# Small loads of the first stage issued behind the first weights, and one square sum moved to ScalarE

## Chip, cores and metric

The kernel runs on one core of one Trainium2 chip. The metric is the time of one execution in device microseconds (us); the median of several runs is quoted. TensorE is called PE, VectorE DVE, ScalarE ACT, GpSimd POOL, and SyncE, which issues the transfers, SP.

## The reference

A trunk of two residual layers over 256 tokens of width 1024. Only the start of it matters here:

```python
cond = jax.nn.silu(c)
cos_b, sin_b = rope_tables(positions, MOBA_DH)      # rotary tables, 64 frequencies
cos_c, sin_c = rope_tables(positions, MLA_ROPE)     # 32 frequencies
mod = cond @ mod_w[layer] + mod_b[layer]            # six vectors of 1024
sh1, sc1, g1, sh2, sc2, g2 = jnp.split(mod[:, None, :], 6, axis=-1)
h = rmsnorm(x, norm_mix[layer]) * (1.0 + sc1) + sh1
y = hybrid_mixer(h, ...)                            # h @ w_in, convolution, gated DeltaNet, attention
x = x + g1 * y
...
```

rmsnorm needs the sum of squares of every token's row. After the mixer each layer has a large expert stage (PEER), which takes most of the time and which nothing here touches.

## The kernel before, in words

Tokens lie in two tiles of 128 partitions (`self.x[:, 0]` and `self.x[:, 1]`). The **first stage** computes the squares (line 1723), the norm, and the shift and scale vectors, in four quarters `q` of the width. A quarter loads two blocks of the modulation matrix with `mods` (1 MB each, line 1696, tile `mw`, six buffers) and one block of the input weights with `fetch` (1 MB, line 790, tile `wraw`, two buffers). DVE reduces the modulation blocks (line 353). Each weight block is split into a high part `whi` by ACT and a low part `wlo` by DVE (both line 131); `quarter` makes the normalised activations `hT` (lines 234 to 250), and PE multiplies three times for each product (lines 135 to 137).

`small` is a 64 KB load of biases and gains. `sincos` (lines 886 to 917), called twice, loads frequencies and positions with four small transfers (lines 895, 896) and reduces the angles with 50 instructions on POOL (lines 898 to 916). What it returns are the Sin activations (line 917), four instructions on ACT, which are issued after the last quarter, ahead of the **hybrid stage** (the mixer). There ACT also evaluates the convolution taps (line 1117) and splits the small gate weights `t<-t` that PE multiplies first with an 8-wide stationary operand.

In the first stage SP, PE, DVE and ACT run in the order in which the code is written. In the hybrid stage a scheduler puts the instructions of each engine in order by its own estimate of when their inputs are ready; so what is written in the first stage also moves the order of the hybrid stage. Each engine executes its own list strictly in that order. Reducing the modulation blocks of later sub-layers (line 353, tile `raw`, three buffers, loaded at line 365) is spread over the hybrid stage. SP has eight semaphores for transfers that it uses in turn, so a transfer is issued only when the eighth before it has landed.

Of the kernel before, what the change touches and what calls it, by code (L numbers as in the profile page):

```python
# [16 lines left out]
OP = mybir.AluOpType  # L17
AX = mybir.AxisListType

P = 128  # L20
D = 1024
KD = D // P
S = 256
TT = S // P
# [43 lines left out]
class Trunk:  # L68
# [222 lines left out]
    def tail(self, products, add, nxt, tmp):  # L291


        def run(g):
            for _ in g:
                pass
        run(products(0, 0))
        run(products(0, 1))
        run(add(0, 0))
        run(add(0, 1))  # L300
        nxt.norm(0)
        run(products(1, 0))
        p = products(1, 1)
        next(p)
        squares = add(1, 0)
        next(squares)
        nxt.turn(0)
        run(p)
        nxt.make(0, tmp, squares)
        run(add(1, 1))  # L310
# [1330 lines left out]
    def run(self, out):  # L1641
        nc = self.nc
        self.hp = self.ctx.enter_context(self.pool("h"))
        self.st = self.ctx.enter_context(self.pool("st", side="right"))
        right, late = ExitStack(), ExitStack()
        self.order = ExitStack()
        start = ExitStack()
        start.enter_context(self.in_order("SP", "PE", "DVE", "Activation"))
        self.consts()

        def open_weights(sets):
            self.sets = sets
            self.wp = right.enter_context(self.pool(f"wp{self.n}", side="right"))

        def before_mla():
            open_weights(2)
            ml = late.enter_context(self.pool("ml0", side="right"))
            self.gate = self.t(ml, [P, D])
            mods = self.mods_in(ml, 2, *((1, p) for p in range(3, 5)))

            def ready():
                r.early = [self.weights(self.a["w1"][:, c * 2048:c * 2048 + 2048], KD, 256) for c in (2, 0)]
                r.early.append(self.load(self.a["w1"][:, 2048:4096], WMAX))
            return mods, ready

        def before_end():
            def ready():
                nc.sync.dma_start(self.fnorm, self.a["final_norm"][None, :].to_broadcast([P, D]))
            ml = late.enter_context(self.pool("ml1", side="right"))
            self.gate, self.fnorm = (self.t(ml, [P, D]) for _ in range(2))  # L1670
            return iter(()), ready

        open_weights(3)
        r = Bag()
        with self.pool("hc") as hc:
            r.row = self.t(hc, [P, D])
            r.cs = self.t(hc, [P, TT, 2, 64])
            r.cw = self.t(hc, [P, 12, 4])
            r.onorm = self.t(hc, [P, P])
            r.wba = self.t(hc, [P, KD * 8])  # L1680
            r.small = self.t(hc, [P, 2, 4])
            e = self.entry(0, 0, self.ss4)
            cond = self.t(hc, [P, KD])
            nc.sync.dma_start(cond, self.a["condc"])
            for i in range(TT):
                nc.sync.dma_start(self.x[:, i], self.a["x"][i * P:(i + 1) * P])
            nc.scalar.activation(cond, cond, AF.Silu)
            self.row_of(r.row, cond)
            with self.pool("mod") as mp, start:
                def tmp():  # L1690
                    return self.t(mp, [P, 512], tag="ent", bufs=4)

                def mods(q, c, pm=None):

                    w = self.t(mp, [P, 2, D], tag="mw", bufs=6)
                    nc.sync.dma_start(w, self.a["mod0"][q, c // 8])
                    self.mod_tile(0, c, w[:, 0], r.row)
                    if pm is None:
                        self.mod_tile(0, c + 1, w[:, 1], r.row)
                        return  # L1700
                    for k in range(KD):
                        nc.tensor.matmul(pm[:, c // 8:c // 8 + 1], w[:, 1, k * P:(k + 1) * P], cond[:, k:k + 1],
                                         start=k == 0, stop=k == KD - 1)

                def bias(c, pm=None):
                    self.mod_bias(0, c, 2 if pm is None else 1)
                    if pm is not None:
                        nc.vector.tensor_add(self.modc[0][:, c + 1:c + 2], pm[:, c // 8:c // 8 + 1],
                                             self.modb[:, 0, c + 1:c + 2])

                def product(ps, c, j, w, q):
                    f = self.proj_n if c >= 2 else self.proj_t
                    n = (256,) if c >= 2 else ()
                    f(ps, w, e.hT, KD, *n, j, ks=range(2 * q, 2 * q + 2), w0=2 * c)

                def products(q, cs):
                    for c in cs:
                        for j in range(2):
                            product(sums[c], c, j, w, q)

                for i in range(TT):
                    sq = self.t(mp, [P, D], tag="sq")
                    nc.vector.scalar_tensor_tensor(sq, self.x[:, i], 1.0, self.x[:, i], op0=OP.mult, op1=OP.mult,
                                                   accum_out=self.ss4[:, i, :1])
                e.norm(0, 1)
                e.turn(0, (0,))
                e.turn(1, (0,))
                sums = [self.out_t() for _ in range(4)]
                w = None
                for q in range(4):  # L1730
                    pm = self.ps()
                    mods(q, 8 + 2 * q, pm)
                    if not q:
                        nc.sync.dma_start(self.small, self.a["small"])
                        turns = self.sincos(r.cs, 64, self.a["freq_b"]) + self.sincos(self.cs1, 32, self.a["freq_c"])
                    else:
                        products(q - 1, (1, 2, 3))
                    if q < 3:
                        w, steps = self.fetch(self.a["w0start"][q], KD, 256)
                        for f in steps:  # L1740
                            f()
                    mods(q, 2 * q)
                    bias(2 * q)
                    bias(8 + 2 * q, pm)
                    if q == 3:
                        w, steps = self.fetch(self.a["w0start"][q], KD, 256, 4)
                    last = e.quarter(q, tmp)
                    if q < 3:
                        products(q, (0,))
                    if q == 1:  # L1750
                        e.turn(0, (1,))
                        e.turn(1, (1,))
                for f in steps:
                    f()
                early = [(Begun(sums[c], lambda j, c=c: j or products(3, (c,))), []) for c in range(4)]
                nc.sync.dma_start(r.wba, self.a["w0ba"])
                nc.sync.dma_start(r.cw, self.a["conv"])
                nc.sync.dma_start(r.small, self.a["gdn_small"][None].to_broadcast([P, 2, 4]))
                nc.sync.dma_start(r.onorm, self.a["o_norm"][None, :].to_broadcast([P, P]))
                early.append(self.fetch(self.a["w0"][6], KD, 256))  # L1760
                early.append(self.fetch(self.a["w0"][5], KD, 256))
            with self.pool("hybrid") as m, self.tc.issue_after(last[0].ins), self.tc.issue_after(last[1].ins):
                for f in turns:
                    f()
                e1 = self.entry(0, 1, self.ss4)
                first = self.hybrid(m, e.hT, r, early, self.mods(r.row, self.raw, (0, 2), (0, 3), (0, 4)), self.ss4, e1)
        e2 = self.entry(1, 0, self.ss2)
        self.peer(0, e1, first, right, ((0, 5), (1, 0)), ((1, 1), (1, 2)), before_mla, e2, self.ss2)
        late.close()
        e3 = self.entry(1, 1, self.ss4)  # L1770
        with self.pool("mla") as m:
            first = self.mla(m, e2, r.early, self.cs1, self.ss4, e3)
        end = self.finish(out)
        self.peer(1, e3, first, right, ((1, 5),), (), before_end, end, self.ss2)
        end.norm(1)
        self.order.close()
        late.close()
        right.close()
# [112 lines left out]
```

## Time and profile before

| | us |
|---|---|
| median of 3 runs | 1911.29 (1910.82 to 1915.98) |
| the profiled execution | 1913.79 |
| its span in the trace | 1912.0 |
| PE busy | 1875.2 (98%) |
| DVE busy | 1532.6 (80%) |
| ACT busy | 951.4 (50%) |
| POOL busy | 51.4 (3%) |

The span runs from the first to the last instruction in the trace; 1.8 us of the profiled execution lie around it. A share of busy time is a mean over all stages: PE at 98% is still idle for most of the first 22 us.

### The profile page before, as it was taken

The numbers are of one execution on the slowest core, as the hardware profiler recorded it, in microseconds if no ns is written. First come the engines' busy times: TensorE is split into PE (matmuls) and PEld (weight loads), VectorE is DVE, ScalarE is ACT, GpSimd is POOL, SyncE is SP. The second block draws the span as 40 slices with busy tenths as digits, with TensorE's granted clock in tenths as the row PEclk, the third lists the DMA queues.
The fourth block names the chain that finished last, engine by engine and source line by source line (L and its number), as shares of the span: only waits on it lengthen the run. The fifth ranks groups of instructions, "written<-read, shape, count | busy, mean of one in ns | idle before, by whom it ended". The sixth has DMA issues, their size and how long they took to land.

```text
span 1912.0 us, 36008 instructions
## 1 busy us (share of the span) xinstructions
PE 1875.2 (98%) x14368; PEld 1716.0 (90%) x14368; DVE 1532.6 (80%) x3265; ACT 951.4 (50%) x1309; POOL 51.4 (3%) x131
## 2 busy tenths in 40 slices
PE   6999999999999999999999999999999999999998
PEld 6999899999999888877879899999999988888886
DVE  7879789998987789878657668999778878985565
ACT  3866555454444444445545765545444444444453
POOL 7000000000000000000000000000000000000000
PEclk9999999999999999999999999999999999999999
DMA  8556575558755555589742445565554555556573
GB/s 324 177 177 236 194 276 187 200 192 281 243 173 175 174 176 175 176 279 325 231 150 111 153 184 204 180 207 186 179 177 169 175 178 177 175 182 199 192 229 102
DMA packets 97080, 376.67 MB, mean 197 GB/s; under 512 B 11920, under 2 KB 12176, under 8 KB 90256
## 3 DMA queue, kind: packets, MB, share of 16 engines
q1 hardware_dynamic: 96912, 374.37, 57.4%
q8 instruction: 112, 1.84, 0.4%
q14 instruction: 56, 0.46, 0.1%
HBM read 373.28 MB, written 1.05 MB: 196 GB/s over the span
## 4 chain that ended last, share of the span: by engine, by line
PE 77%; DVE 10%; DMA 7%; ACT 4%; issue 2%; SPq 0%; ACTq 0%; DVEq 0%
PE ps L783 26%; PE ps L626 21%; PE ps L628 11%; DMA raw<-in_v_dram 4%; DVE lo L131 3%; PE ps L649 3%; PE ps L135 3%; PE ps L137 3%; PE ps L136 3%; DMA t<-in_modT_dram 2%; PE ps L736 1%; ACT hi L131 1%; DVE t L353 1%; PE ps L323 1%; PE ps L1207 1%
## 5 line engine op out<-in xcount | busy, mean ns | idle before, releaser
L131 ACT CAST hi<-raw 128x1024 fp32r<-128x1024 f32 x508 | 534.4, 1054 | 741.8 <-PE ps L626 301.1
L131 DVE TENSOR_TENSOR lo<-raw,hi 128x1024 fp32r<-128x1024 f32 x508 | 619.2, 1221 | 233.6 <-ACT hi L131 231.0
L626 PE MATMUL ps<-hT,hi 128*128 128x256 f32 x4096 | 513.1, 278 | 2.0 <-ACT hi L131 2.0
L626 PEld LDWEIGHTS ps<-hT,hi 128*128 128x128 f32 x4096 | 484.6, 188 | 2.5 <-ACT hi L131 2.4
L628 PE MATMUL ps<-hT,lo 128*128 128x256 f32 x2048 | 275.7, 277 | 1.3 <-DVE lo L131 1.2
L783 PE MATMUL ps<-hi,vwh 128*128 128x512 f32 x976 | 266.5, 394 | 2.9 <-ACT hi L131 2.6
L783 PE MATMUL ps<-lo,vwh 128*128 128x512 f32 x976 | 261.8, 390 | 0.4 <-DVE lo L131 0.3
L783 PE MATMUL ps<-hi,vwl 128*128 128x512 f32 x976 | 261.3, 389 | 0.0
L628 PEld LDWEIGHTS ps<-hT,lo 128*128 128x128 f32 x2048 | 251.9, 188 | 2.6 <-DVE lo L131 2.3
L783 PEld LDWEIGHTS ps<-lo,vwh 128*128 128x128 f32 x976 | 182.6, 188 | 40.5 <-DVE lo L131 2.8
L783 PEld LDWEIGHTS ps<-hi,vwl 128*128 128x128 f32 x976 | 183.2, 188 | 38.9
L783 PEld LDWEIGHTS ps<-hi,vwh 128*128 128x128 f32 x976 | 180.1, 188 | 40.8 <-ACT hi L131 5.7
L131 DVE TENSOR_TENSOR wlo<-wraw,whi 128x1024 fp32r<-128x1024 f32 (+1 forms) x84 | 99.1, 1203 | 40.3 <-ACT whi L131 40.3
L645 DVE TENSOR_TENSOR ohG<-ohB,t 128x512 f16<-128x512 f16 x256 | 98.6, 416 | 0.0
L131 ACT CAST whi<-wraw 128x1024 fp32r<-128x1024 f32 (+1 forms) x84 | 83.7, 1032 | 29.8 <-PE ps L137 8.7
L135 PE MATMUL ps<-hT,whi 128*128 128x256 f32 x288 | 84.0, 292 | 7.0 <-ACT hT L246 6.6
L639 DVE TENSOR_TENSOR ohA<-t,t 128x1024 f16<-128x1024 f16 x128 | 87.4, 683 | 0.0
L137 PE MATMUL ps<-hT,wlo 128*128 128x256 f32 x288 | 82.1, 286 | 0.0
L136 PE MATMUL ps<-hT,whi 128*128 128x256 f32 x288 | 82.0, 285 | 0.0
L353 DVE SCALAR_TENSOR_TENSOR t<-t 128x1024 f32<-128x1024 f32 x56 | 67.3, 1220 | 17.8 <-DMA t<-in_modT_dram 12.2
L649 PE MATMUL ps<-ohG,ohA 128*128 128x64 f16 x2048 | 79.0, 193 | 0.3 <-DVE ohG L645 0.2
L649 PEld LDWEIGHTS <-ohA 128*128 128x128 f16 x2048 | 67.3, 97 | 12.2 <-issue 8.7
(480 smaller groups left out, 2253.9 us busy)
## 6 DMA issues: line engine op xcount, KB each, us to landing
raw<-in_uT_dram SPq DMA_DIRECT2D x256, 512.0 KB, 3.3
raw<-in_v_dram SPq DMA_DIRECT2D x256, 512.0 KB, 3.7
t<-in_modT_dram SPq DMA_DIRECT2D x56, 512.0 KB, 5.5
wraw<-in_w_dram SPq DMA_DIRECT2D x13, 1024.0 KB, 6.8
raw<-in_modT_dram SPq DMA_DIRECT2D x24, 512.0 KB, 4.4
wraw<-in_wq_dram SPq DMA_DIRECT2D x12, 1024.0 KB, 6.0
mw<-in_mod_dram SPq DMA_DIRECT2D x8, 1024.0 KB, 13.6
wraw<-in_w0start_dram SPq DMA_DIRECT2D x4, 1024.0 KB, 11.8
```

Of the source, the lines that this page charges most:

```text
L131: return self.nc.scalar.copy(hi, src), self.nc.vector.tensor_sub(lo, src, hi.bitcast(F32))
L135: mm(out, l[0], r[0], start=start, stop=False)
L136: mm(out, l[0], r[1], start=False, stop=False)
L137: mm(out, l[1], r[0], start=False, stop=stop)
L323: mm(ps[g][:, i], e.hT[:, s, k, sl], w[:, b, k, :], start=s + k + b == 0, stop=s == 1 and n == KD - 1)
L353: self.nc.vector.scalar_tensor_tensor(w, w, 1.0, row, op0=OP.mult, op1=OP.mult, accum_out=self.modc[layer][:, c:c + 1])
L626: mm(pair, hi[:, k], hT[:, s, k], start=k == 0 and s == 0, stop=False)
L628: mm(pair, lo[:, k], hT[:, 0, k], start=False, stop=k == KD - 1)
L639: nc.vector.tensor_tensor(A, self.iota_t[:, None].to_broadcast(full), pairs(0, full), op=OP.is_equal)
L645: nc.vector.tensor_tensor(B[:, j], b0, pairs(2 + j, part), op=OP.mult)
L649: nc.tensor.matmul(ps[:, t], A[:, t // 2, :, t % 2], B[:, j, t // 2, :, t % 2], start=j == 0, stop=j == 1)
L783: self.nc.tensor.matmul(acc[i][c], w[a][:, j, i * P:(i + 1) * P], v[b][:, c * 512:(c + 1) * 512], start=first and j + a + b == 0, stop=False)
```

## The change

The 64 KB load `small` and the four small loads of `sincos` were issued right behind the first modulation block, ahead of the first weights. Now `small` is issued behind the first quarter's weights and its second modulation block, and the `sincos` calls, with their loads and their POOL instructions, stand in the second quarter behind its loads. The squares of the second token tile are summed by ACT (`square_sum`, line 191) in place of DVE.

```diff
-                for i in range(TT):
-                    sq = self.t(mp, [P, D], tag="sq")
-                    nc.vector.scalar_tensor_tensor(sq, self.x[:, i], 1.0, self.x[:, i], op0=OP.mult, op1=OP.mult,
-                                                   accum_out=self.ss4[:, i, :1])
+                sq = self.t(mp, [P, D], tag="sq")
+                nc.vector.scalar_tensor_tensor(sq, self.x[:, 0], 1.0, self.x[:, 0], op0=OP.mult, op1=OP.mult,
+                                               accum_out=self.ss4[:, 0, :1])
+                self.square_sum(mp, self.ss4[:, 1, :1], self.x[:, 1])
...
                     mods(q, 8 + 2 * q, pm)
-                    if not q:
-                        nc.sync.dma_start(self.small, self.a["small"])
-                        turns = self.sincos(r.cs, 64, self.a["freq_b"]) + self.sincos(self.cs1, 32, self.a["freq_c"])
-                    else:
+                    if q:
                         products(q - 1, (1, 2, 3))
                     if q < 3:
                         w, steps = self.fetch(self.a["w0start"][q], KD, 256)
                         for f in steps:
                             f()
                     mods(q, 2 * q)
+                    if not q:
+                        nc.sync.dma_start(self.small, self.a["small"])
+                    if q == 1:
+                        turns = self.sincos(r.cs, 64, self.a["freq_b"]) + self.sincos(self.cs1, 32, self.a["freq_c"])
                     bias(2 * q)
```

On SP, at the start of the program, the transfers stood in this order before (`mw` are modulation blocks, `wraw` input weights, `lo` the work tile of `sincos`):

```order
L1696 DMA mw_171<-in_mod_dram 128x2048
L1734 DMA t_70<-in_small_dram 128x128
L895 DMA lo_183<-in_freq_b_dram 128x64
L896 DMA lo_183<-in_pos_dram 128x2
L895 DMA lo_211<-in_freq_c_dram 128x32
L896 DMA lo_211<-in_pos_dram 128x2
L790 DMA wraw_239<-in_w0start_dram 128x2048
L1696 DMA mw_247<-in_mod_dram 128x2048
```

In the changed kernel the same place on SP reads:

```order
L1696 DMA mw_171<-in_mod_dram 128x2048
L790 DMA wraw_182<-in_w0start_dram 128x2048
L1696 DMA mw_190<-in_mod_dram 128x2048
L1741 DMA t_70<-in_small_dram 128x128
L1696 DMA mw_223<-in_mod_dram 128x2048
L790 DMA wraw_270<-in_w0start_dram 128x2048
L1696 DMA mw_278<-in_mod_dram 128x2048
L895 DMA lo_282<-in_freq_b_dram 128x64
L896 DMA lo_282<-in_pos_dram 128x2
L895 DMA lo_310<-in_freq_c_dram 128x32
L896 DMA lo_310<-in_pos_dram 128x2
```

The first weights moved ahead by five small transfers; the four transfers of `sincos` moved behind five more blocks of 1 MB. POOL's own list keeps its order.

On ACT, from the end of the first stage on, the changed kernel has these rows (`t_100` and `t_85` are the rotary tables, `t_639` the gate weights, `hi_572` a convolution's work tile):

```order
L131 CAST whi_517<-wraw_515 128x512 x4
L917 ACTIVATE t_100<-lo_282 128x2x64 x2
L917 ACTIVATE t_85<-lo_310 128x2x32 x2
L131 CAST t_639<-t_103 128x64
L1117 ACTIVATE hi_572<-ps_166,t_101 128x256
L1051 ACT_TABLE_LOAD
```

The Sin activations stand at the same place as before, directly behind the last weights' high parts and ahead of everything that the hybrid stage asks of ACT. Some twenty rows on, ACT before read:

```order
L1123 ACTIVATE qkv_560<-hi_597 128x512
L1038 COPY k_104_667<-ps_642 8x256
L1126 ACTIVATE lo_619<-qkv_560 128x512
L1047 ACT_TABLE_LOAD
L1047 ACTIVATE t_689<-t_687 128x8
L1056 ACTIVATE t_697<-t_697 128x8
L131 CAST whi_738<-wraw_736 128x1024
L1062 ACT_TABLE_LOAD
```

and it now reads:

```order
L1038 COPY k_104_667<-ps_642 8x256
L131 CAST whi_548<-wraw_546 128x1024
L1047 ACT_TABLE_LOAD
L1047 ACTIVATE t_689<-t_687 128x8
L1123 ACT_TABLE_LOAD
L1123 ACTIVATE qkv_560<-hi_597 128x512
L1056 ACT_TABLE_LOAD
L1056 ACTIVATE t_697<-t_697 128x8
L1126 ACTIVATE lo_619<-qkv_560 128x512
L131 CAST whi_738<-wraw_736 128x1024
L1062 ACT_TABLE_LOAD
```

A convolution's activation (line 1123) now stands between two gate activations, and two table loads came in with it. On DVE, in the same part of the program, three reductions of modulation blocks (line 353) that stood some 80 rows later now stand ahead of the gates' small steps; this is the piece in the changed kernel:

```order
L1049 RECIPROCAL t_689<-t_689 128x8
L929 TENSOR_TENSOR ropf_133_768<-ps_740,t_100 128x128
L353 SCALAR_TENSOR_TENSOR raw_1168,t_86<-raw_1168,t_99 128x1024
L353 SCALAR_TENSOR_TENSOR raw_1229,t_86<-raw_1229,t_99 128x1024
L353 SCALAR_TENSOR_TENSOR raw_1283,t_86<-raw_1283,t_99 128x1024
L1058 TENSOR_SCALAR t_700<-t_697 128x8
L930 TENSOR_TENSOR lo_741<-rope_132_767,ropf_133_768 128x2x64
```

The three rows of line 353 came in there; before, none of these three stood ahead of `L1058`. Further on the difference is the other way round: between the first attention row (line 949) and the first row of line 1320 DVE had twelve rows of line 353 before and has five now.

## Rows read from the trace of the kernel before

**Rows 1.** The chain of waits, first stage and late hybrid: start us, us, what.
```profile
5.28 8.83 DMA wraw<-in_w0start_dram
...
17.69 2.39 DVE mw L353 x4
...
22.16 0.58 PE ps L135
...
156.38 5.82 DMA raw<-in_wq_dram
```
**Rows 2.** Timeline of SP's queue: start us, us, line, what it issues.
```profile
2.12 0.43 SPq L1696 DMA_DIRECT2D mw<-in_mod_dram  x1
2.59 0.43 SPq L1734 DMA_DIRECT2D t<-in_small_dram  x1
3.07 0.66 SPq L895 DMA_DIRECT2D lo<-in_freq_b_dram  x1
...
4.80 0.44 SPq L896 DMA_DIRECT2D lo<-in_pos_dram  x1
...
9.19 0.63 SPq L790 DMA_DIRECT2D wraw<-in_w0start_dram  x1
```
**Rows 3.** DMA issues: count, KB each, median us from issue to landing.
```profile
t<-in_small_dram SPq DMA_DIRECT2D x1, 64.0 KB, 6.4
...
lo<-in_freq_b_dram SPq DMA_DIRECT2D x1, 32.0 KB, 7.1
lo<-in_pos_dram SPq DMA_DIRECT2D x2, 1.0 KB, 6.7
```
**Rows 4.** The tile mw, the transfer issued at 2.12 us.
```profile
DMA to landing us min/median/max: 6.7/6.7/6.7
```
**Rows 5.** The tile wraw, the transfer issued at 9.19 us.
```profile
DMA to landing us min/median/max: 12.4/12.4/12.4
```
**Rows 6.** Waits in the first 60 us: us in total, times, longest us.
```profile
DVE wlo L131 <- ACT whi L131: 3.6, 1, 3.6
```
**Rows 7.** The tile sq: duration ns min/median/max, first and last start us, forms.
```profile
L193 ACT ACTIVATE sq<-lat x4: 432/532/634, 1024.8 to 1031.4; 128x256 f32<-128x256 f32 x2, 128x512 f32<-128x512 f32 x2
...
L1723 DVE SCALAR_TENSOR_TENSOR sq<-t x2: 1225/1226/1227, 5.1 to 6.4; 128x1024 f32<-128x1024 f32 x2
```
**Rows 8.** Timeline of POOL, 8 to 60 us: first, two middle and last of 50.
```profile
10.39 1.28 POOL L898 CAST lo<-lo 128x2 f32<-128x2 int32 x1 [9.32 <-DMA lo<-in_pos_dram]
...
26.65 1.49 POOL L915 TENSOR_SCALAR lo<-lo 128x128 f32<-128x128 f32 x1
...
45.30 0.53 POOL L916 TENSOR_SCALAR lo<-lo 128x128 f32<-128x128 f32 x1
...
49.06 0.37 POOL L916 TENSOR_SCALAR lo<-lo 128x64 f32<-128x64 f32 x1
```
**Rows 9.** Timeline of DVE beside it.
```profile
26.34 1.30 DVE L353 SCALAR_TENSOR_TENSOR mw<-mw,t 128x1024 f32<-128x1024 f32 x1
```
**Rows 10.** Timeline of ACT, 50 to 75 us.
```profile
50.37 0.80 ACT L917 ACTIVATE t<-lo 128x128 f32<-128x128 f32 x4
52.45 0.47 ACT L1117 ACTIVATE hi<-ps,t 128x256 f32<-128x256 f32 x1 [1.28 <-PE ps L137]
...
64.31 1.28 ACT L1047 ACT_TABLE_LOAD   x1
...
74.77 0.21 ACT L1082 ACTIVATE t<-t 128x8 f32<-128x8 f32 x1
```
**Rows 11.** Timeline of PE: a product in the second quarter, the first with gate weights.
```profile
32.86 0.41 PE L137 MATMUL ps<-whi,hT 128*128 128x256 f32 x1
...
54.52 0.28 PE L135 MATMUL ps<-hT,t 128*8 128x256 f32 x1
```
**Rows 12.** Stretches: us, then PE, PEld, DVE, ACT, POOL busy (instructions), granted clock, DMA share, GB/s.
```profile
60.00:70.00 10.00, 9.24 (x77) 8.81 (x76) 9.49 (x29) 9.63 (x17) 0.00 (x0) 1.00 0.81 271
...
147.00:200.00 53.00, 51.79 (x365) 46.73 (x364) 49.10 (x94) 29.56 (x49) 6.71 (x38) 1.00 0.68 242
```

## The prediction

> **What bounds the kernel now.** I read the chain of waits first. In the first stage it runs from the first weights' load (issued at 5.28 us, landed at 14.1) over ACT's and DVE's split of them and DVE's modulation sums to the first product of PE at 22.16 us [rows 1]. From there the pieces of the chain are PE's until the hybrid stage. So the landing of the first weights sets the first 22 us, and whatever lets PE start earlier moves all that follows, as long as nothing stops PE again.
>
> Next, SP's queue. The transfers land in the order of issue. The first modulation block lands at 2.12 + 6.7 = 8.8 us [rows 2, 4], `small` at 2.59 + 6.4 = 9.0, the first frequencies at 3.07 + 7.1 = 10.2, the last positions at 4.80 + 6.7 = 11.5 [rows 2, 3], and then the weights at 14.1. The second weights land at 9.19 + 12.4 = 21.6 [rows 2, 5] with two modulation blocks between: three blocks in 7.5 us, 2.5 us for 1 MB. So 11.5 + 2.5 = 14.0 is the first weights' landing, and the five small loads, 114 KB in all, hold the queue for 11.5 - 8.8 = 2.7 us.
>
> Third, POOL. Its 50 instructions for the angles run from 10.39 us, when the positions have landed, to 49.06 + 0.37 = 49.4 [rows 8]: 39 us. One on 128x128 takes 0.53 us at 45.30 and one on 128x64 0.37 at 49.06, but the one at 26.65 us takes 1.49, beside a DVE reduction of 1.30 us that began just before it [rows 8, 9]: while DVE runs a long instruction with two inputs from SBUF, POOL gets about one instruction done for each of DVE's. ACT's Sin activations come at 50.37 us, 1 us after POOL's last; ACT then waits 1.28 us for PE until 52.45 [rows 10]. In the kernel before, POOL is thus just in time, with about 3 us to spare.
>
> **The change, part by part.** The squares: DVE loses one instruction of 1.23 us, ACT gains one of about 1.1 us (estimate: 0.43 us for 256 and 0.63 for 512 columns, so 0.2 more for each 256) [rows 7]. The norm still needs both tiles, and DVE idles 3.6 us before the first weights' split [rows 6], which hides either sign. If that idle time were gone, it would be worth 1.2 us at most. I take 0.
>
> The first weights: they stand directly behind the first modulation block, so they land at 8.8 + 2.5 = 11.3 instead of 14.1, and the second modulation block at 13.8. Everything up to the first product moves by 2.8 us, to about 19.4: a gain of 2.8 us, if PE goes on as before. Bounds: 0 (the queue is held by something else) to 3.2 (POOL is idle then, so DVE's splits meet no neighbour).
>
> The Trainium skill weighs against this gain: "DMA: Bandwidth & Descriptors", section "Anatomy of one DMA", says that the fixed 2 us of a transfer is mostly completion and that only bytes at 436 GB/s scale, by which 114 KB would hold the queue some 0.3 us (an estimate from that page), and the gain would be 0.3. The row measures 2.7 [rows 2 to 4], and I go by the row.
>
> POOL's start: the four `sincos` loads are now behind five more blocks, so the positions land at 8.8 + 5 x 2.5 + about 1.5 = 22.8 us, against 10.4. POOL starts at about 23.0, 12.6 us later, and all of it now lies in the stretch where DVE is full. That is the term that decides. In the kernel before, POOL's last 31 instructions, from 26.65 us on, took 22.8 us [rows 8], 0.74 each. DVE will be where it was 2.8 us later, so up to 46.6 us POOL does about 23.6 / 0.74 = 32 of its 50. DVE's last four half-size splits (to about 49.1) let four more through. Then DVE stands, since its next row needs ACT's part of the gate weights, which stands behind the Sin activations. The 14 left go at the free pace, 0.37 us for the narrow and 0.53 for the wide ones [rows 8], with the gaps between some 0.55 on average (an estimate): 7.7 us. POOL ends at 49.1 + 7.7 = 56.8, and ACT is free at about 57.4. Lower bound: the 18 left at 46.6 all at 0.44, so 54.5. Upper bound: all 50 at the 0.78 of before, so 62.
>
> Behind the Sin activations on ACT are queued the gate weights' high part, the first convolution taps and all later weights' high parts; PE and DVE wait for these. PE's first product with gate weights was at 54.52 [rows 11] and would be due at 51.7; it comes at about 57.8. ACT's first tap moves from 52.45 to about 57.6: **5.1 us late**, the gain of 2.8 already in.
>
> The order behind it: between 57 and 80 us ACT has two more table loads, 1.28 us each [rows 10], 2.6 us. DVE has three more reductions of line 353, 1.2 us each (the four rows of the chain are two of them with their readouts, 2.39 us [rows 1]), 3.6 us, ahead of the gates' steps. Both engines were full there, DVE 9.49 and ACT 9.63 of 10 us [rows 12]. They run side by side, so the larger counts, less what DVE idled before: I take 3.0 (bounds 0, if PE has other work, and 6.2, if they add). The gates' activation at 74.77 [rows 10] then comes at about 83, **8.1 us late**.
>
> What comes back: further on DVE has seven reductions fewer between the first attention row and the norm of the mixer, some 8 us, and the chain's wait of 5.82 us for a load that stood behind those reductions [rows 1] should go. But in that stretch PE is busy 51.79 of 53 us [rows 12]: an earlier input gives PE at most the 1.2 us that it idles, and as much again in short waits that the modelled ends hide. I take 1.5 of these (bounds 0 and 5).
>
> **Sum.** +5.1 + 3.0 - 1.5 = +6.6 us. The profiled execution took 1913.8 (span 1912.0 and 1.8 around it), which would become 1920.4. The median is 2.5 us lower, 1911.3; on it the forecast is 1917.9, **1918 us**. About 0.3% (5.7 us) is what a measurement of this kernel can tell from no change, so this lies just outside.
>
> **Rivals.** *POOL is in time* (the other side). The point that decides is POOL's last instruction against 49.65 us, when ACT's first tap would be due. If the loads overtake the blocks, or POOL's instructions shrink to their free 0.44 us, 23 + 22 = 45 us is early enough, nothing stands, and 2.8 us are won: 1908.5, or 1911 where the three reductions still cost. For it: the narrow instructions at the free pace. Against: all landings in order of issue, and the 0.74 us under a full DVE.
>
> *The stall is paid back later.* DVE is relieved in the late hybrid stage and the 5.82 us wait disappears; if PE's small waits there hold 5 us and not 1.5, the net is +1 to +4: 1914. For it: the chain runs over DVE and that load there. Against: PE is 98% busy in it.
>
> *PE's clock falls in the stall.* A product of 256 columns took 0.41 us in the second quarter and 0.28 later [rows 11], the levels of 1.2 and 2.4 GHz, although the profile grants 1.00 of both. At 32.9 us, 10.7 us behind its first product, PE had not yet gone up. If the 6 us of idleness bring the lower level back, some 60 products cost up to 0.13 us more, half of it beside waits: +4, so 1922. The Trainium skill ("TensorE: Matmul & The Clock Gate", "HAM oscillation") states that a long idle stretch throttles the clock again. By that rule this rival is the likely one; no idle stretch of that length stands in this trace behind the first stage, and DVE, not PE, sets the pace up to 80 us, so I leave it a smaller chance.
>
> **How the numbers follow.** Forecast 0.46 (of it 0.30 above +5.7 us and 0.16 below), paid back later 0.26, POOL in time 0.10, clock 0.14, and 0.04 for a new order of the hybrid stage that wins 6 us. Slower by over 0.3%: 0.30 + 0.14 + 0.06 from the first two at their upper bounds = 0.50. Faster: 0.04 and 0.02 of POOL in time = 0.06. Same: 0.44. The forecast alone goes from +3 to +10. The range takes in most of the paid-back case and of the clock: 1910.5 to 1923.
>
> **What would show it.** Right: the first weights issued at about 2.6 us and landed near 11.3, PE's first product near 19.4, POOL from 23 to 57, the Sin activations ending near 57.4, a hole of some 6 us on PE in front of the gate weights, two more table loads on ACT before 85 us. Wrong: POOL starting before 20 us, or finishing before 50; no hole on PE; the rows at the end of the hybrid stage (the squares at 200 us) at the same place as before or earlier.

## The result, and the profile after

The changed kernel takes 1925.34 us, the median of 6 runs (1923.71 to 1930.13), beside 1913.73 (1910.82 to 1915.98) of the kernel before: the ratio is 1.0059, 95% interval 1.0048 to 1.0070, or 11.3 us slower. In a second set of runs it was 1.0065 (1.0047 to 1.0082). The forecast of 1918 had the sign; the time lies 2.3 us above the upper end of its range. The profiled execution has a span of 1924.5 us at a mean granted clock of 0.994, before 1912.0 and 0.999.

The first weights did what they should. SP's queue in the kernel after (start us, us, what; [rows 2] answer to it):

```profile
2.59 0.43 SPq L790 DMA_DIRECT2D wraw<-in_w0start_dram  x1
...
13.97 0.33 SPq L896 DMA_DIRECT2D lo<-in_pos_dram  x1
```

The weights go out at 2.59 us and no longer at 5.28 [rows 1], the last positions at 13.97 and not at 4.80 [rows 2]. The price stands on POOL and on ACT (timelines; [rows 8, 10] before):

```profile
22.45 0.68 POOL L898 CAST lo<-lo 128x2 f32<-128x2 int32 x1 [21.39 <-DMA lo<-in_pos_dram]
...
55.05 0.37 POOL L916 TENSOR_SCALAR lo<-lo 128x64 f32<-128x64 f32 x1
```

```profile
11.41 1.99 ACT L131 CAST whi<-wraw 128x1024 fp32r<-128x1024 f32 x2 [0.51 <-DMA wraw<-in_w0start_dram]
...
47.04 0.30 ACT L917 ACTIVATE t<-lo 128x128 f32<-128x128 f32 x1
51.91 0.46 ACT L917 ACTIVATE t<-lo 128x128 f32<-128x128 f32 x2 [4.57 <-POOL lo L916]
55.45 0.26 ACT L917 ACTIVATE t<-lo 128x64 f32<-128x64 f32 x1 [3.09 <-POOL lo L916]
55.75 0.47 ACT L1117 ACTIVATE hi<-ps,t 128x256 f32<-128x256 f32 x1
```

ACT splits the first weights at 11.4 us, and PE's first product comes at 19.23 in place of 22.16 [rows 1]. But POOL ends at 55.4 us and not at 49.4. ACT, which works its queue in order, waits twice for it, 7.7 us together, and the first tap (line 1117) comes at 55.75, 3.3 us late. Behind ACT wait DVE and then PE. The waits between 44 and 60 us (engine line and what it waited for: us, times, longest):

```profile
ACT t L917 <- POOL lo L916: 7.7, 2, 4.6
DVE t L131 <- ACT t L131: 7.1, 1, 7.1
...
PE ps L135 <- ACT t L131: 4.7, 1, 4.7
```

The windows (us, then busy time of PE, PEld, DVE, ACT, POOL, granted clock, DMA share, GB/s) show the hole, and that it isn't the only one. Before, the clock is 1.00 in every one of these stretches ([rows 12] for 60 to 70 us):

```profile
50.00:60.00 10.00, 5.28 (x32) 4.13 (x32) 3.84 (x10) 4.97 (x13) 4.74 (x13) 0.83 0.48 197
60.00:70.00 10.00, 8.74 (x71) 7.91 (x70) 9.91 (x24) 9.58 (x14) 0.00 (x0) 1.00 0.60 209
70.00:80.00 10.00, 7.73 (x42) 7.27 (x42) 7.87 (x25) 5.96 (x10) 0.00 (x0) 0.67 0.89 303
90.00:100.00 10.00, 7.37 (x55) 7.11 (x53) 9.36 (x26) 5.03 (x8) 2.56 (x2) 0.86 0.42 165
```

Last, the new order. ACT between 66 and 75 us, and DVE beside it:

```profile
66.73 1.28 ACT L1047 ACT_TABLE_LOAD   x1
...
68.25 1.28 ACT L1123 ACT_TABLE_LOAD   x1
...
70.20 1.28 ACT L1056 ACT_TABLE_LOAD   x1
...
73.17 1.28 ACT L1062 ACT_TABLE_LOAD   x1
```

```profile
69.84 1.22 DVE L353 SCALAR_TENSOR_TENSOR raw<-raw,t 128x1024 f32<-128x1024 f32 x1
70.98 1.22 DVE L353 SCALAR_TENSOR_TENSOR raw<-raw,t 128x1024 f32<-128x1024 f32 x1
72.13 1.22 DVE L353 SCALAR_TENSOR_TENSOR raw<-raw,t 128x1024 f32<-128x1024 f32 x1
73.27 0.17 DVE L1058 TENSOR_SCALAR t<-t 128x8 f32<-128x8 f32 x1
...
87.20 1.22 DVE L353 SCALAR_TENSOR_TENSOR raw<-raw,t 128x1024 f32<-128x1024 f32 x1
88.56 0.68 DVE L1173 TENSOR_TENSOR t<-t,ps 128x512 f32<-128x512 f32 x1
89.16 1.22 DVE L353 SCALAR_TENSOR_TENSOR raw<-raw,t 128x1024 f32<-128x1024 f32 x1
```

A Silu (line 1123) now stands between two exponentials (lines 1047 and 1056): two more table loads. On DVE three reductions of line 353 stand together ahead of the gates' step of line 1058, and two more on either side of line 1173.

What waits behind them shows in three rows. Ahead of the gates' activation (line 1082) stands a split of weights on ACT; before, it waited 1.8 us for its load, and now it waits 4.0 us for PE, in the stretch with the granted clock of 0.67. The first row is before, the second after:

```profile
71.46 1.99 ACT L131 CAST whi<-wraw 128x1024 fp32r<-128x1024 f32 x2 [1.77 <-DMA wraw<-in_w_dram]
```

```profile
79.97 1.99 ACT L131 CAST whi<-wraw 128x1024 fp32r<-128x1024 f32 x2 [3.98 <-PE ps L137]
```

Further on PE waits 2.6 us for DVE, which is busy 9.36 of the 10 us from 90 on:

```profile
97.52 0.58 PE L136 MATMUL ps<-wlo,hT 128*128 128x256 f32 x1 [2.63 <-DVE wlo L131]
```

### The profile page after: what moved, and what is told of

It is laid out like the page before. It is cut to its first block, busy times and chain, and to the rows that moved or that the text cites. A ratio compares the mean times of both kernels' runs of the same rounds, so it can differ in the third digit from the quotient of the medians.

```text
span 1924.5 us, 36011 instructions
## 1 busy us (share of the span) xinstructions
PE 1882.0 (98%) x14368; PEld 1724.1 (90%) x14368; DVE 1533.2 (80%) x3263; ACT 955.3 (50%) x1313; POOL 48.1 (2%) x131
## 4 chain that ended last, share of the span: by engine, by line
PE 81%; DVE 7%; DMA 5%; ACT 3%; issue 1%; ACTq 0%; SPq 0%; DVEq 0%
PE ps L783 29%; PE ps L626 23%; PE ps L628 11%; PE ps L649 3%; PE ps L135 3%; PE ps L136 3%; PE ps L137 3%; DMA raw<-in_v_dram 3%; DVE lo L131 2%; PE ps L736 1%; ACT hi L131 1%; PE ps L1207 1%; PE ps L456 1%; DMA t<-in_cond_dram 1%; PE ps L323 1%
## 5 line engine op out<-in xcount | busy, mean ns | idle before, releaser
L649 PEld LDWEIGHTS <-ohA 128*128 128x128 f16 x2048 | 67.3, 97 | 11.7 <-issue 8.5
```

What stands on the lines that cost most here:

```text
L649: nc.tensor.matmul(ps[:, t], A[:, t // 2, :, t % 2], B[:, j, t // 2, :, t % 2], start=j == 0, stop=j == 1)
```

## The experiments

Theories: *stall*, the time that ACT waits for POOL goes to the end; *order*, the new order of the hybrid stage costs time without any stall; *clock*, PE's lower granted clock behind the holes carries a large part. A time in us is the measured ratio less 1, times the median of before on that chip (1913.7 to 1916.4). The places compared are, for each trace, the start of one instruction less its start in the trace of before. The last two rows are not differences: they are PE's idle time between its first product and the first product of line 323, and what the lower clock took there (busy time times one less the granted clock, added up over stretches of 1 to 2 us; an estimate). The trace of before is a favourable one: its mean granted clock is 0.999, as in 17 of the 80 other runs of that kernel, whose mean is 0.9975. So the places in the other traces come out a little late by it, and the timed runs decide on sizes. In the edits, loops and helper tiles that stand on one line in the kernels are written out or left out.

| start, us, of | before | after | after, 2nd trace | e_pool_more | e_stall_long | e_pool_short | the same, 2nd trace | e_tables | e_reductions | e_angles_q0_42 |
|---|---|---|---|---|---|---|---|---|---|---|
| first tap, L1117 (ACT) | 52.45 | +3.30 | +2.78 | +2.71 | +9.23 | -4.06 | -3.37 | +0.50 | -0.36 | -3.09 |
| table load of L1047 (ACT) | 64.31 | +2.42 | +1.91 | +2.70 | +9.22 | -5.02 | -4.34 | +0.51 | -0.35 | -3.09 |
| table load of L1062 (ACT) | 66.88 | +6.29 | +5.78 | +2.78 | +9.20 | -1.15 | -0.47 | +4.75 | +0.58 | -3.10 |
| gates' activation, L1082 (ACT) | 74.77 | +8.50 | +7.13 | +3.40 | +10.05 | +1.06 | +0.88 | +2.21 | +2.62 | -2.35 |
| inverse's first copy, L1195 (ACT) | 84.71 | +10.12 | +8.82 | +3.39 | +10.06 | +2.68 | +2.57 | +1.65 | +6.83 | -2.35 |
| first product of L323 (PE) | 206.20 | +14.22 | +11.81 | +2.92 | +10.40 | +6.74 | +5.54 | +5.65 | +6.75 | -2.74 |
| timed, us | | +11.3 | +12.4 | +2.9 | +8.4 | +3.1 | | +4.4 | +4.0 | -2.5 |
| PE idle up to line 323, us | 3 | 13 | 12 | 6 | 10 | 8 | 8 | 5 | 4 | 2 |
| taken by the lower clock, us | 0.0 | 8.0 | 6.0 | 0.0 | 3.2 | 6.4 | 3.3 | 1.6 | 6.8 | 1.7 |

**e_pool_more: the stall alone.** In `sincos` of the kernel before:

```
+            for _ in range(6 * j * (half == 32)):
+                ve.tensor_scalar(t, r, 1.0, None, op0=OP.mult)
+                ve.tensor_copy(r, t)
```

> The kernel before, with its loads, its squares and the order of its instructions on ACT, DVE and PE unchanged; only POOL gets 12 instructions more on 128x64 (a product by 1 and a copy), ahead of the last Sin activation. Stall theory (a late POOL alone carries the loss): POOL's last instruction at about 55 us in place of 49.4, ACT's first tap about 3 to 4 us late, a hole on PE of 3 to 5 us, and the time +3 to +8 us, the more if PE's granted clock falls behind the hole. Order theory (only the new order of the hybrid stage, with its table loads and early reductions, costs time): 0 to +2 us, the hole being taken up by later idle time.

Measured: 1.0015 (1.0006 to 1.0024). The trace has the wait of the changed kernel, in the order of the kernel before:

```profile
49.77 0.65 ACT L917 ACTIVATE t<-lo 128x128 f32<-128x128 f32 x3
54.99 0.26 ACT L917 ACTIVATE t<-lo 128x64 f32<-128x64 f32 x1 [4.57 <-POOL lo L916]
55.16 0.46 ACT L1117 ACTIVATE hi<-ps,t 128x256 f32<-128x256 f32 x1
```

The tap is 2.7 us late, the end of the stage 2.9, the timed runs 2.9. PE waits 1.7 us there, its granted clock stays 1.00, and nothing is added and nothing given back. That speaks for the stall theory at its lower end: this stall costs its own length (the interval of the timed runs is 1.1 to 4.6 us).

**e_pool_short: the new order alone.** In `sincos` of the changed kernel:

```
-            for k, c in enumerate((c1, c2, c3)):
+            for k, c in enumerate((c1 + c2 + c3,)):
```

> The changed kernel, order on ACT, DVE and PE unchanged, but POOL does 16 instructions fewer: the reduction of the angles takes one step in place of three, so the sines are less exact. POOL should end at 44 to 48 us in place of 55.4. Stall theory: no hole on PE, granted clock 1.00, and the gain of 2.9 us at the first product is kept as far as the new order allows: 1908 to 1914 us, that is 12 to 17 below the changed kernel. Order theory: the two table loads and three early reductions still cost 5 us or more by the gates' activation: 1917 to 1922. Clock theory (a third of the loss is PE's lower clock after the hole): in between, near 1914, with the granted clock telling.

Measured: 1.0016 (1.0007 to 1.0025), 1919.92 us. POOL ends at 46.8 us, in time, and the tap comes early:

```profile
46.54 0.80 ACT L917 ACTIVATE t<-lo 128x128 f32<-128x128 f32 x4
48.39 0.47 ACT L1117 ACTIVATE hi<-ps,t 128x256 f32<-128x256 f32 x1 [0.92 <-PE ps L137]
```

But the 4.1 us won at the tap are gone by the gates' activation. From the table load of line 1047 to that of 1062, 3.9 us are lost, just as in the changed kernel (from +2.4 to +6.3). So the two kernels differ by the stall: 7.4 us at the tap, 11.3 - 3.1 = 8.2 us in the timed runs. The order costs the rest, with or without a stall; the lower clock that comes with it, 6.4 us of PE's time in this trace, is part of that cost. The pure stall theory (1908 to 1914) falls; the order theory had it (1917 to 1922).

**e_pool_short_again: how much of that is one execution.**

> The same kernel as e_pool_short, for a second trace: its profiled execution was 8 us above that of before, its timed runs only 3 us above theirs. If PE's granted clock between 65 and 100 us differs from one execution to the next, the shift of the last inverse step's copies (7.0 us against before in the first trace) will come out smaller or larger here by 2 to 6 us, at the places where the clock was 0.63 to 0.85; if the clock falls are the same each time, it will come out at 7.0 again, within 0.3.

Stretches of the first trace, and then of the second:

```profile
60.00:70.00 10.00, 7.51 (x47) 6.92 (x47) 9.91 (x32) 8.44 (x12) 0.00 (x0) 0.81 0.88 325
...
90.00:100.00 10.00, 9.92 (x61) 9.87 (x61) 7.19 (x24) 4.54 (x8) 0.00 (x0) 0.66 0.55 201
```

```profile
60.00:70.00 10.00, 7.52 (x50) 6.78 (x50) 9.91 (x32) 9.12 (x12) 0.00 (x0) 0.91 0.93 325
...
90.00:100.00 10.00, 9.81 (x73) 9.60 (x74) 8.57 (x25) 5.80 (x11) 0.00 (x0) 0.83 0.58 208
```

The holes come again, the clock does not to the same extent: 0.91 and 0.83 in place of 0.81 and 0.66. The inverse's first copy of line 1210 comes 5.6 us late and not 7.0, a little less of a change than was expected, and the span is 1916.2 in place of 1920.1. A single trace of this kernel is good for about 4 us of span.

**e_tables and e_reductions: what in the order costs.** Both are the kernel before, in `gdn_gates`:

```
e_tables
+        nc.scalar.activation(scr, e, AF.Silu)
         nc.scalar.activation(e, e, AF.Exp)
e_reductions
         nc.scalar.activation(e, e, AF.Exp)
+        for _ in range(9):
+            nc.vector.scalar_tensor_tensor(scr, r.row[:, :256], e[:, 0, :1], r.row[:, :256], op0=OP.mult, op1=OP.mult)
```

> The kernel before, loads and POOL as they were, with one small Silu activation (128x8, its result unread) set between the gates' two first exponentials, which forces the two additional table loads of the changed kernel at their place. The scheduler then also brings two reductions of line 353 forward, ahead of the gates' steps, as in the changed kernel. No stall by POOL. Order theory: 2.6 to 3.5 us on ACT up to the logarithm's table load, and some of it kept to the end: +2 to +6 us, the more if PE's granted clock falls in the holes. Rival (ACT and DVE of the hybrid stage have slack for it, the stall alone costs): 0 to +1 us.

> The kernel before, loads and POOL as they were, with nine DVE products of 256 columns (their results unread, about 0.47 us each, 4.2 us together) behind the gates' second exponential, between the gates' steps and the rope products, in place of early reductions; no additional table loads. Order theory with DVE as its carrier: the gates' activation of line 1082 comes 2 to 4 us late and +2 to +4 us stay at the end. Rival (DVE's work there is hidden, ACT's table loads carry the cost): 0 to +1 us.

Measured: 1.0023 (1.0014 to 1.0032) and 1.0021 (1.0010 to 1.0033), +4.4 and +4.0 us, both within what the order theory gave (+2 to +6 and +2 to +4). ACT in e_tables:

```profile
64.82 1.28 ACT L1047 ACT_TABLE_LOAD   x1
...
66.34 1.28 ACT L1056 ACT_TABLE_LOAD   x1
...
68.80 1.28 ACT L1056 ACT_TABLE_LOAD   x1
```

Two table loads, with the two reductions that follow them, cost 4 us with the small loads and POOL untouched, at a granted clock of 1.00 up to 147 us. But the loss is 1.65 us at the inverse and 5.65 at line 323: the larger part arises between 126 and 200 us, where the changed kernel loses nothing more, and by what wait was not tracked down. So the run shows that two loads there can cost 4 us, not that they cost it in the changed kernel by the same wait.

In e_reductions 4 us of DVE work without a table load cost as much, but what carries it stays open between DVE and the clock. The granted clock fell to 0.50 from 65 to 70 us, as in e_square (below), though the added work starts only at 67.8; ACT's split ahead of the gates' activation waits for PE, and what the lower clock took up to line 323 (6.8 us) is as much as the whole delay there:

```profile
65.00:70.00 5.00, 5.00 (x25) 5.00 (x25) 3.81 (x15) 3.92 (x7) 0.00 (x0) 0.50 0.78 279
```

```profile
73.52 2.00 ACT L131 CAST whi<-wraw 128x1024 fp32r<-128x1024 f32 x2 [2.81 <-PE ps L137]
```

In the timed runs the mean granted clock of e_reductions is 0.9958, of e_tables 0.9972, of before 0.9974.

**e_angles_q0 and e_angles_q0_42: the weights first, without the rest.** In the changed kernel, and for the second also in `sincos`:

```
-                    if q == 1:
+                    if not q:
                         turns = self.sincos(...) + self.sincos(...)
e_angles_q0_42, besides
-            ve.tensor_scalar(n, n, magic, None, op0=OP.add)
-            ve.tensor_scalar(n, n, -magic, None, op0=OP.add)
+            ve.tensor_scalar(n, n, magic, -magic, op0=OP.add, op1=OP.add)
...
-                ve.tensor_scalar(t, n, -c, None, op0=OP.mult)
+                ve.tensor_scalar(t, n, -c, 0.0 if k else add, op0=OP.mult, op1=OP.add)
...
-            ve.tensor_scalar(r, r, add, lim, op0=OP.add, op1=OP.min)
-            ve.tensor_scalar(r, r, -lim, None, op0=OP.max)
+            ve.tensor_scalar(r, r, lim, -lim, op0=OP.min, op1=OP.max)
```

> The changed kernel with the loads of the angles one quarter earlier, behind the second modulation block and in front of the third: the first weights stay early, POOL starts at about 16.5 us (10.4 before, 22.5 in the changed kernel), and the order on ACT, DVE and PE is that of the kernel before. Stall theory: POOL ends at about 49 to 52 us, so ACT's first tap comes at 50 to 52.5 and little or nothing of the 2.9 us is lost: 1908.5 to 1912. Theory that the later loads themselves cost time (small, positions or the blocks behind them): 1915 or more, with POOL in time.

> The kernel of the run e_angles_q0 (weights first, the angles' loads behind the second modulation block), with POOL's work for the angles written in 42 instructions in place of 50: two-step instructions for the rounding, the shift by a quarter turn and the two limits; the values are the same but for rounding. The order on ACT, DVE and PE is that of the kernel before. Stall theory: POOL ends at about 47 us in place of 51, no wait on ACT, the first tap at about 48.5 in place of 52.45, and the whole gain of some 4 us is carried to the end: ratio 0.997 to 0.9985 to the kernel before. Rival (the gain is eaten in the hybrid stage, where DVE and ACT are full): 0.999 to 1.000.

Measured: 0.9995 (0.9985 to 1.0004) and 0.9987 (0.9978 to 0.9996). ACT in e_angles_q0, and then in e_angles_q0_42:

```profile
51.01 0.26 ACT L917 ACTIVATE t<-lo 128x64 f32<-128x64 f32 x1 [2.78 <-POOL lo L916]
51.17 0.46 ACT L1117 ACTIVATE hi<-ps,t 128x256 f32<-128x256 f32 x1
```

```profile
47.78 0.80 ACT L917 ACTIVATE t<-lo 128x128 f32<-128x128 f32 x4
49.36 0.47 ACT L1117 ACTIVATE hi<-ps,t 128x256 f32<-128x256 f32 x1 [0.78 <-PE ps L137]
```

Both keep the order of the kernel before, and POOL starts at 15.4 and 15.9 us. With 50 instructions it ends at 51.0, ACT waits 2.8 us for it, and more than half of the gain at the tap is lost; with 42 it ends at 45.0 with 2.8 us to spare, and 3.1 us at the tap become 2.7 at line 323 and 2.5 in the timed runs. That is the version that beats both kernels, 1913.01 beside 1915.98 us. It also speaks against the theory that moving the small loads costs something by itself.

**e_square: the squares alone.** In the kernel before, only the squares of tile 1 on ACT, as in the change.

> The kernel before with the squares of the second tile on ACT, nothing else; the order on all engines otherwise that of before. Theory that the squares are hidden in DVE's idle time ahead of the first weights' split: 0, within 1 us. Rival (ACT's square comes in front of the modulation path or delays the first split): +0.5 to +1.2 us, with the first product on PE later than 22.16 us.

Measured: 1.0003 (0.9994 to 1.0012), PE's first product at 22.06. The squares are hidden. Its trace nevertheless ends 2.5 us above that of before, and shows where: with the order unchanged and the same idleness of PE, the granted clock falls, and the gates' activation comes 2.4 us late:

```profile
60.00:65.00 5.00, 4.25 (x34) 4.03 (x33) 5.00 (x12) 4.98 (x10) 0.00 (x0) 0.91 0.75 238
65.00:70.00 5.00, 5.00 (x25) 5.00 (x25) 3.33 (x14) 4.22 (x7) 0.00 (x0) 0.50 0.81 265
```

The same two stretches of the kernel before:

```profile
60.00:65.00 5.00, 4.26 (x38) 4.04 (x36) 5.00 (x12) 4.98 (x10) 0.00 (x0) 1.00 0.75 242
65.00:70.00 5.00, 4.98 (x41) 4.77 (x42) 4.49 (x19) 4.65 (x8) 0.00 (x0) 1.00 0.86 300
```

**e_cs1_late: half of POOL's work moved out of the way.** In the changed kernel `sincos(r.cs, ...)` alone stays at its place, and in `before_mla`:

```
+            for f in self.sincos(self.cs1, 32, self.a["freq_c"]):
+                f()
```

> The changed kernel, but the second table of angles (two loads, 25 instructions of POOL, two Sin activations), which only the last layer reads, is made after the hybrid stage. POOL has 25 instructions from 22.5 us on and should end near 40. The scheduler's order of the hybrid stage is then near that of before: no additional table loads, 14 early reductions in place of 17 to 21. Stall theory and order theory agree here: no stall and no reordering, the front 3 to 5 us ahead of before, and 0 to 2.6 us for two table loads later on: ratio 0.998 to 1.000, that is 11 to 14 us below the changed kernel. Theory that moving the small loads costs time by itself (later loads of small or positions in front of weights): 1.003 or more.

Measured: 1.0039 (1.0025 to 1.0052), outside what the stall and order theories gave and, by the number alone, in the range of the theory that the later loads cost time; the trace shows another cause. The tap comes 2.4 us early (3 to 5 were expected), and no table load came in. Line 323 is 1.2 us late all the same: PE idles no longer up to there than before (2 us beside 3), but the lower clock takes 5.1 us, with 0.72 and 0.59 granted in the two stretches of 5 us from 60 to 70. Then the moved work stalls another place. Its waits between 825 and 850 us:

```profile
ACT t L917 <- POOL lo L916: 10.4, 2, 6.8
DVE lo L131 <- ACT t L917: 9.8, 1, 9.8
...
PE ps L783 <- DVE lo L131: 7.8, 1, 7.8
```

The two Sin activations stand there in ACT's queue before POOL's 25 instructions have run, and the values' low parts and PE's products wait behind them: 7.8 us on PE, where the timed runs lose 7.5 in all.

**e_warm and e_warm_again: the clock kept up in the hole.** In `gdn_gates` of the changed kernel, ahead of the gate products:

```
+        warm = self.ps()
+        for k in range(12):
+            nc.tensor.matmul(warm, hT[:, 0, k % 8, :P], hT[:, 0, 2 * (k % 4):2 * (k % 4) + 2], start=True, stop=True)
```

> The changed kernel with 12 products of 512 columns more on PE, whose sums nobody reads, in front of the gate weights' products, where PE stands for some 5 us. The order on ACT and DVE is unchanged. Clock theory (the fall of PE's granted clock after the hole costs 3 to 5 us): the granted clock stays nearer 1.00 between 55 and 110 us and the time falls by 2 to 5 us against the changed kernel, to 1920 to 1923. Stall theory and order theory: the clock costs nothing by itself since ACT and DVE set the pace there, so 0 to +2 us against the changed kernel, 1925 to 1927.

> The same kernel as e_warm (the changed kernel with 12 products of 512 columns in the hole), for a second set of times: its first trace came out below the changed kernel's, its first times did not. Clock theory: 1.003 to 1.005 of before, with a mean granted clock over the timed runs above the 0.995 of the changed kernel. Otherwise 1.006 to 1.007 again.

Measured: 1.0065 (1.0052 to 1.0079) and 1.0053 (1.0035 to 1.0071), beside 1.0059 and 1.0065 of the changed kernel: no difference that these intervals of some 3 us can show. In the first trace the hole is filled, and the granted clock stays at 1.00 up to 60 us:

```profile
50.00:55.00 5.00, 4.09 (x24) 3.29 (x22) 0.00 (x0) 0.46 (x2) 4.33 (x12) 1.00 0.93 380
...
60.00:65.00 5.00, 2.21 (x11) 1.67 (x10) 5.00 (x8) 4.64 (x8) 0.00 (x0) 0.74 0.38 107
```

From 60 us on PE then only waits longer, 2.8 of the 5 us, since ACT (4.64) and DVE (5.00) set the pace. What the clock took there, waiting takes now. Up to the gates it is otherwise. There the clock is 1.00, not 0.67, and ACT waits 1.3 us for PE and not 4.0:

```profile
70.00:80.00 10.00, 9.06 (x76) 8.47 (x75) 9.37 (x35) 8.59 (x12) 0.00 (x0) 1.00 0.90 305
```

```profile
77.36 1.99 ACT L131 CAST whi<-wraw 128x1024 fp32r<-128x1024 f32 x2 [1.33 <-PE ps L137]
```

The gates' activation comes 5.9 us late in this trace (8.5 and 7.1 in those of the changed kernel, 7.3 in e_warm_again), line 323 10.6 us (14.2, 11.8, 13.0). In the timed runs the filled hole gave back about half of the clock (mean 0.9964 and 0.9962 beside 0.9948 and 0.9952), so the pair does not price the clock.

**e_stall_long and e_stall_long_warm: a long stall, empty and half filled.** As e_pool_more, with 14 in place of 6, and for the second 16 products as in e_warm.

> As e_pool_more, with 28 instructions more on POOL in place of 12: loads and the order on ACT, DVE and PE are those of the kernel before, and POOL should end at 60 to 62 us, ACT's first tap some 8 to 10 us late, behind a hole of some 8 us on PE. Theory that a stall costs its own length and no more: the same 8 to 10 us at the end, and a granted clock as in before. Clock theory (a hole of this length brings the lower clock, and products at it cost more): 10 to 14 us at the end, with a mean granted clock over the timed runs some 0.001 to 0.002 below that of before.

> The same as e_stall_long, with 16 products of 512 columns on PE, whose sums nobody reads, in front of the gate weights' products, that is in the hole; order on DVE as in before, on ACT but for two rows. Clock theory: with the hole half filled the granted clock stays nearer that of before, and the time is 1 to 4 us below e_stall_long. If a stall costs only its own length: the same as e_stall_long within 1.5 us.

Measured: 1.0044 (1.0028 to 1.0061) and 1.0046 (1.0028 to 1.0065), +8.4 and +8.8 us, for taps that come 9.2 and 9.0 us late. The first has a hole of 6.9 us on PE and a granted clock of 0.50 from 60 to 65 us:

```profile
62.32 0.38 PE L135 MATMUL ps<-hT,t 128*8 128x256 f32 x1 [6.93 <-ACT t L131]
```

The mean clock of the first is 0.0014 below that of before, as the clock theory had it, and with the hole half filled it rises from 0.9963 to 0.9975 (6 runs each); the time doesn't fall. A stall costs about its own length, cold or warm, as far as intervals of some 3 us can tell.

**e_after_again: the changed kernel once more.**

> The changed kernel itself, for a second trace and times beside the same runs of before as the other two. Up to the gates' activation of line 1082 the places should be those of the first trace within 0.5 us, but for the stretches in which the granted clock was below 1.00; if the clock varies from one execution to the next, the inverse's copies of line 1210, 14.3 us late in the first trace, come out 11 to 15 us late here. Time 1.005 to 1.007 of before.

Measured: 1.0065 (1.0047 to 1.0082), and the places in the table: some 0.5 us less up to the table load of line 1062, 1.4 us less at the gates' activation, where the clock of 70 to 80 us was 0.83 in place of 0.67, and 11.85 at line 1210.

## Why the prediction failed: point by point

- **The squares, 0.** Right (e_square).
- **The first weights, a gain of 2.8.** Right: 19.23 us for the first product where 19.4 was said; e_angles_q0_42 carries 2.5 of it to the end. The 0.3 us that the prediction worked out from the Trainium skill ("DMA: Bandwidth & Descriptors", section "Anatomy of one DMA") is refuted by the 2.9 us of this trace. That section gives its figures for transfers that GpSimd issues, and these are issued by SP, so it is the use of the figure that fails.
- **POOL's end and ACT's stall.** Right in mechanism and chain, a little too large: POOL ended at 55.4 and not 56.8, the tap is 3.3 us late (2.8 in the second trace) and not 5.1. As a term of its own (the lateness against the tap that the weights would have allowed) it was forecast at 2.8 + 5.1 = 7.9 us; e_pool_short puts it at 7.4 in the trace and 8.2 in the timed runs.
- **The order, "I take 3.0 (bounds 0, if PE has other work, and 6.2, if they add)", less 1.5 that comes back.** This is the step that failed. Net it was forecast at +1.5. The timed runs give 5.6: e_pool_short at +3.1 against e_angles_q0_42 at -2.5, both with POOL in time and the weights first, differ mainly by the order. Up to the gates' activation the 3.0 was too small: from the tap on the order took 5.2 us in the changed kernel (4.4 in the second trace) and 5.1 (4.3) in e_pool_short. "They run side by side, so the larger counts" was itself right up to the table load of line 1062: the three reductions ran beside the table loads (69.8 to 73.3 us), and ACT's own rows made the 3.9 us there. What the term put at nothing is PE: behind the waits it ran at the lower clock, and ACT waited 4.0 us for it; in e_warm, with that clock at 1.00, the order takes 2.9 us from the tap to the gates (4.1 in e_warm_again). The worse part is what was to come back. Not 1.5 us came back; between the gates and line 323 another 4.7 to 5.7 us were lost in each of the six traces with this order. The two reductions beside line 1173 delay the inverse (from +8.5 us at the gates to +10.1 at its first copy), PE then waits 2.6 us for DVE's low parts, and a lower clock takes 3.2 and 1.7 us up to line 1210 in the two traces; behind that nothing more is lost or won (+14.3 at line 1210, +14.2 at line 323). How much of the 5.6 us is waiting and how much the clock, the timed runs don't tell.
- **The gates' activation, 8.1 us late.** It came 8.5 and 7.1 us late. That the number was right is luck: the stall was smaller and the order dearer than said. What lay behind it was priced as a gain of 1.5 and was a loss.
- **The sum.** -2.5 + 8.2 + 5.6 = 11.3 us, against the forecast's -2.8 + 7.9 + 3.0 - 1.5 = 6.6. The first of these is measured; the other two are differences between timed kernels, uncertain by some 2 to 3 us each. The forecast also stood on a median of three runs, 1911.29, that became 1913.73 with three more: 2.4 of the 7.4 us by which it was too low.
- **The rivals.** *POOL is in time* was wrong about this kernel, and right about its point that decides: in e_angles_q0_42, where POOL ends at 45.0, the gain is 2.5. *Paid back later* is refuted (e_pool_more, e_stall_long). *The clock falls in the stall* came true as a fact, with a granted clock of 0.83 from 50 to 60 us and 0.67 from 70 to 80, where the forecast had given it a chance of 0.14. The Trainium skill states that a long idle stretch throttles the clock again ("TensorE: Matmul & The Clock Gate", "HAM oscillation"), and the hole of 4.7 us agrees with that. In e_square the clock fell without such a hole. Its price of 4 us is neither confirmed nor refuted: the lower clock took 8.0 and 6.0 us of PE's time up to line 323 in the two traces, part of it in place of waits.
- **The range** ended 11.7 us above the median of 1911.3 on which it stood. The measured medians differ by 11.6. So the time lies above the range by no more than the shift of that median, while the forecast within it missed by the order's term.

What stays open is the clock's share. Each run lists its granted clock: the mean is 0.9948 for the changed kernel (6 runs) and 0.9975 for the one before (80 runs). Within before, the 36 runs at 0.997 have a mean span of 1914.7 us and the 17 at 0.999 one of 1913.05, which would make the difference of 0.0027 worth 2.2 us (an estimate), and the intervals of the filled and empty pairs don't exclude that. Not tried was to hold the order of before in the changed kernel itself; the stall in that order was made with POOL's work alone.

## What to carry to other kernels

A helper engine that is just in time is a bound in waiting: before its inputs are moved behind bulk loads, count its instructions at the pace that it really has beside its neighbours, and price what stands behind the instruction that waits for it, since such a stall went to the end here at about its own length. Moving the wait elsewhere moves the stall (e_cs1_late); fewer helper instructions and loads placed right behind the last urgent block win (e_angles_q0_42). Where a change lets the scheduler reorder a stage in which two engines are both full, price also the engine that waits behind them, and give nothing back without a row that shows who waits; and take two traces before a difference of a few us is read from one.

## What was not expected of the hardware

- The granted clock of one stretch differs between executions of the same or nearly the same order: from 65 to 70 us 1.00 in the kernel before and 0.50 in e_square, with PE busy 4.26 and 4.25 of 5 us just before; it cost that trace 2.4 us by the gates' activation; the median of the timed runs doesn't show it.
- What a lower clock costs depends on who waits: from 60 to 65 us of e_warm PE stands 2.8 of 5 us even at a granted clock of 0.74, behind ACT and DVE; between 70 and 80 us ACT waits for PE, 4.0 us at 0.67 in the changed kernel and 1.3 us at 1.00 in e_warm, in the same order of ACT's and DVE's instructions.
- POOL gains more from fewer instructions than their free time: 8 of 50 less brought its end from 51.0 to 45.0 us, 0.75 us each, the pace beside a busy DVE and not the 0.37 to 0.53 of [rows 8].
